# Second feed-forward output, parts 1 to 3: seven block products of 256 columns in place of plain 512-column products

## The chip, the cores and the metric

The kernel runs on one core of one Trainium2 chip. The metric is the device time of one execution in microseconds, as the median over runs of the same program. The engines are named as in the profile: PE (TensorE, with its weight loads as PEld), DVE (VectorE), ACT (ScalarE), POOL (GpSimd) and SP (SyncE, which here only issues DMAs).

## What is computed

The reference is one decoder block: a gated feed-forward, a token-mixing layer, a second gated feed-forward and a final norm, for 512 tokens of width 1024, in float32. What matters here is the second feed-forward:

```python
def swiglu(u, w_in, w_out):
    a, b = jnp.split(u @ w_in, 2, axis=-1)
    return (jax.nn.silu(a) * b) @ w_out

u = modulate(rmsnorm(h, g_norm_ffn2[l]), sh3, sc3)
h = h + 0.5 * gt3 * swiglu(u, w_ffn2_in[l], w_ffn2_out[l])
return rmsnorm(h, g_final)
```

The hidden width is 2816, that is 22 tiles of 128 rows; the output is 8 tiles of 128 rows; everything is held transposed, with the 512 tokens as columns.

## The kernel before

**Three matmuls for one.** A float32 product is made of three: each operand is split into a high part, rounded to the matmul's float32 form, and the low remainder. A product is high times high, high times low and low times high (`mm3`, L372 to L377, and L767 to L769 in `product`). The split of a weight chunk of 128 x 1024 is one ACT copy (L331, `whi`) and one DVE subtraction (L343, `wlo`) into a ring that has room for seven chunks. `look(n)` splits chunks up to n ahead of the one that PE takes next, `take` gives PE the next one.

**Block products.** The input half of the feed-forward (`u @ w_in`) runs from tile 4 on as `duo`, which makes two hidden tiles. It views weights, input and output as 2 x 2 blocks (512 rows each of the input, `a` and `b` of the output, 256 tokens each) and makes the product with seven block products in place of eight, by the Strassen-Winograd scheme: PE sums the seven in three PSUM banks A, B and C, ACT copies intermediate sums out (L774), and DVE adds them up (L807, L831). One block product is 24 matmuls of 256 columns and takes one weight chunk. Of the seven chunks of a set four are loaded; two more are sums that DVE makes (L268), and two are made by an adding DMA from POOL (L276), all ordered in `plan` by `blocks`. The sums of the input `u` are made once, as tiles `S`.

**Hidden tiles and parts.** After `duo` come `mult` (silu(a) times b, L793), `high` (ACT, L774, into `HI`) and `low` (DVE, L800, into `HK`). The 22 hidden tiles go into the output product in five parts, `PARTS = ((0, 4), (4, 8), (8, 12), (12, 16), (16, 22))`. The output product of a part is written in `ffn` (L907 to L931): per part 8 output tiles, 4 hidden tiles each, 3 matmuls of 512 columns for each pair, four weight chunks, and for each output tile one DVE operation that multiplies by the gate and adds into `H` (L923). One pair of hidden tiles more than the part needs is made ahead of parts 1 to 3 (`pairs_before`).

**What sets the order.** Each engine's order is written out by hand: `look`, `product`, `step` and the copies follow each other in the program, and `later(n, f)` puts a piece of work behind the n-th block product from now. All weight DMAs are issued from SP in the order of `plan`, as buffers come free. When a block product follows plain 512-column matmuls, `settle` (L381) puts one matmul of 240 columns ahead of it. Eight PSUM banks are there; six are in rotation through `nb()`.

Of the kernel before, what the change touches and what calls it, by code (L numbers as in the profile page):

```python
# [8 lines left out]
F32 = mybir.dt.float32  # L9
# [5 lines left out]
P = 128  # L15
T = 512
# [43 lines left out]
            for i, c in ((0, c0), (0, c1), (1, c1), (1, c0))]  # L60


def lay_ffn(w_in, w_out, first, plain):
# [13 lines left out]
    for k0, k1 in PARTS:  # L77
        for m in range(KT):
            outs.append(_fmajor(w_out[k0 * P:k1 * P], np.arange(m * P, (m + 1) * P)))
    n = KT * (len(PARTS) - 1)  # L80
    return ins, [np.concatenate(outs[i:i + 2], axis=1) for i in range(0, n, 2)] + outs[n:]

# [64 lines left out]
class Kernel:  # L147
# [6 lines left out]
    def plan(self):  # L154
        (i1, o1), mix, (i2, o2) = chunk_widths()
        self.chunks = []
        for name, ws in (("wf1i", i1), ("wf1o", o1), ("wmix", mix), ("wf2i", i2), ("wf2o", o2)):
            off, rec = 0, []
            for w in ws:
                rec.append((name, off, w))  # L160
                off += P * w
            self.chunks.append(rec)
        f1i, f1o, mx, f2i, f2o = self.chunks


        self.loads, self.order, self.last = [], [], {}
        self.shifted, self.adds = set(), {}

        def plain(recs):
            for r in recs:  # L170
                n = len(self.loads)
                self.loads.append(r)
                self.last[n] = len(self.order)
                self.order.append((r[2], n, ("raw", n), None))

        def blocks(recs, plus=False):
            n = len(self.loads)
            i = len(self.order)
            self.shifted.update(range(len(self.order), len(self.order) + 7))
            self.loads.extend(recs)  # L180
            r11, r12, r22, r21 = (("raw", n + i) for i in range(4))
            x0, x1 = ("x", 0), ("x", 1)
            add = OP.add if plus else OP.subtract
            x2 = x1 if plus else x0
            if plus:
                self.adds[i + 2], self.adds[i + 3] = (r12, r22, True), (x1, r21, False)
            for need, src, make in ((0, r11, None), (1, x0, (x0, r12, r11, add)), (2, x1, (x1, r22, x0, add)), (3, r21, None),
                                    (3, r12, (r12, r22, r12, not plus and add)), (3, r22, None),
                                    (3, x2, (x2, r21, x1, not plus and add))):
# [387 lines left out]
    def out_end(self, ms, ksrc, gate):  # L577
# [2 lines left out]
        v, g = nc.vector, nc.gpsimd  # L580
        tiles = {}
        A, Bh = slice(0, HT), slice(HT, T)
        rA, rB = self.B[6], self.B[7]
        self.held = self.pos

        def scaled(m, hs):
# [95 lines left out]

    def ffn_post(self, j, s, pb):
        nc = self.nc
        h = self.fw.tile([P, T], F32, name=("hf", "u3")[j % 2])
        nc.vector.tensor_tensor(h, s, pb, op=OP.mult)
        hh, hl = self.HH[j % NH], self.HL[j % NH]
        nc.scalar.activation(hh, h, AF.Copy)  # L690
        nc.vector.tensor_tensor(hl, h, hh, op=OP.subtract)

    def ffn_silu(self, j, pa):
        s = self.fw.tile([P, T], F32, name=("sl", "u2")[j % 2])
        self.nc.scalar.activation(s, pa, AF.Silu)
        return s

# [73 lines left out]
    def duo(self, n, j, first, last, extra):  # L771
# [13 lines left out]
        s = self.fw.tile([P, 2 * T], F32, name="sl")  # L785
        c = self.fw.tile([P, 2 * T], F32, name="hf")
        u2, u3, p5 = (self.fw.tile([P, T], F32, name=x) for x in ("u2", "u3", "p5"))
# [10 lines left out]
        def low():  # L798
            x = slice(j % NH * T, (j % NH + 2) * T)
            v.tensor_tensor(self.HLall[:, x], c, self.HHall[:, x], op=OP.subtract)  # L800
# [31 lines left out]
        if last:  # L832
            mult()
            high()
            low()
        else:
            self.later(1, mult)
            self.later(2, high)
            self.later(2, low)

    def ffn2(self):
        self.put, self.now = [], 0
        bk = [self.nb() for _ in range(4)]
        self.head(2, bk, AF.Silu)

# [15 lines left out]
        self.ready = True  # L861
        self.free += self.rawx[1:]

    def open_ffn(self):
# [4 lines left out]
        self.HH, self.HL = ([x[:, i * T:(i + 1) * T] for i in range(NH)] for x in (self.HHall, self.HLall))  # L869
        self.Xall = xp.tile([P, 4 * D], F32, name="X")  # L870
        a11, a21, a12, a22 = (self.Xall[:, i * D:(i + 1) * D] for i in range(4))
        self.U4, self.X, self.rawx = ((a11, a12), (a21, a22)), [a11, a21], [a12, a22]
# [11 lines left out]
    def ffn(self, n, j, last=None):  # L884
# [9 lines left out]

        for part, (k0, k1) in enumerate(PARTS):
            tail = part + 1 == len(PARTS)
            extra = 1
            while j < pairs_before(n, part):
                if j < PLAIN[n]:
                    self.ffn_pair(j, beside)  # L900
# [4 lines left out]
                    j += 2  # L905
            if n == 0:
                last = self.beside_out(part) or last  # L907
            nk = k1 - k0
            hk = [(self.HH[k % NH], self.HL[k % NH]) for k in range(k0, k1)]
            if not tail:  # L910
# [674 lines left out]
    def build(self):  # L1585
# [23 lines left out]
        self.cond = tl("cond", D)  # L1609
# [3 lines left out]
        self.cs = tl("cs", 2 * T)  # L1613
        self.cos, self.sin = self.cs[:, :T], self.cs[:, T:]
        tl("pad", 32)
        self.tr, self.pi = tl("tr", 5 * P), tl("pi", P, I32)
        self.B = [psum.tile([P, T], F32, name=f"bank{i}") for i in range(8)]
        self.banks, self.bi = self.B[:6], 0
        self.adat = {}
# [11 lines left out]
            self.ffn(0, FIRST)  # L1631
            self.sums.close()
        self.mix()
        with self.open_ffn() as self.f2:
            self.sums, self.retired = self.open_sums(), []
            self.ffn2()

# [140 lines left out]
def lay_inputs(x, c, positions, w_ada, b_ada, g_norm_ffn1, w_ffn1_in, w_ffn1_out, g_norm_mix, w_in, w_pool,  # L1778
# [4 lines left out]
    f1i, f1o = lay_ffn(A(w_ffn1_in)[0], A(w_ffn1_out)[0], FIRST, PLAIN[0])  # L1783
    f2i, f2o = lay_ffn(A(w_ffn2_in)[0], A(w_ffn2_out)[0], 0, PLAIN[2])
    wp = np.zeros((P, 2 * P), np.float32)
    for g in range(4):
        r = 64 * (g % 2)
# [30 lines left out]
```

## Time and profile before

| what | value |
|---|---|
| median of 3 runs | 992.41 us (991.48 to 993.05) |
| the profiled execution | 992.0 us |
| its span in the profile | 990.2 us |
| around the span | 1.8 us |
| granted PE clock, mean | 0.999 |
| matmuls in the built program | 6500, of which 14 are `settle` |

The profile of this page is of one execution. Busy times count matmuls that overlap each other once; the duration given for a matmul includes its passage through the pipeline, so the pace of a stream of matmuls is read from their starts. For PE, DVE and ACT a "start" of the next row may lie ahead of the end of the row before, too: instructions of one engine overlap a little.

### The profile page before, as it was taken

The numbers are of one execution on the slowest core, as the hardware profiler recorded it, in microseconds if no ns is written. First come the engines' busy times: TensorE is split into PE (matmuls) and PEld (weight loads), VectorE is DVE, ScalarE is ACT, GpSimd is POOL, SyncE is SP. The second block draws the span as 40 slices with busy tenths as digits, with TensorE's granted clock in tenths as the row PEclk, the third lists the DMA queues.
The fourth block names the chain that finished last, engine by engine and source line by source line (L and its number), as shares of the span: only waits on it lengthen the run. The fifth ranks groups of instructions, "written<-read, shape, count | busy, mean of one in ns | idle before, by whom it ended". The sixth has DMA issues, their size and how long they took to land.

```text
span 990.2 us, 16423 instructions
## 1 busy us (share of the span) xinstructions
PE 979.9 (99%) x6688; PEld 892.8 (90%) x6688; DVE 764.6 (77%) x1072; ACT 474.6 (48%) x712; POOL 45.5 (5%) x49
## 2 busy tenths in 40 slices
PE   8999999999999999999999999999999999999997
PEld 7888998989999899888879998998899898998997
DVE  7989979889797677888879877768676667566653
ACT  5453553525445553446545552455355254352553
POOL 0000000000000000006200000000010000000002
PEclk9999999999999999999999999999999999999999
DMA  9856445465563416654243326513576365563512
GB/s 345 277 184 241 150 149 178 163 192 160 186 205 105 141 57 194 229 184 161 68 122 111 107 81 212 175 44 106 145 194 174 88 175 140 128 184 80 152 34 86
DMA packets 47470, 151.19 MB, mean 153 GB/s; under 512 B 6561, under 2 KB 9377, under 8 KB 47394
## 3 DMA queue, kind: packets, MB, share of 16 engines
q1 hardware_dynamic: 44224, 140.18, 43.4%
q0 software_dynamic: 2592, 9.44, 5.5%
q8 instruction: 52, 0.85, 0.4%
q10 hardware_dynamic: 578, 0.53, 0.2%
q14 instruction: 24, 0.20, 0.1%
HBM read 135.29 MB, written 2.24 MB: 139 GB/s over the span
## 4 chain that ended last, share of the span: by engine, by line
PE 94%; DVE 2%; DMA 1%; SPq 1%; issue 1%; ACT 0%; POOL 0%; POOLq 0%; DVEq 0%; ACTq 0%
PE bank L375 15%; PE bank L376 15%; PE bank L377 15%; PE bank L769 13%; PE bank L768 13%; PE bank L767 13%; PE bank L1744 1%; PE bank L1748 1%; PE bank L1746 1%; SPq L1076 1%; PE bank L1420 1%; PE bank L1122 1%; PE bank L1173 1%; DMA H<-xT 1%; PE bank L1421 1%
## 5 line engine op out<-in xcount | busy, mean ns | idle before, releaser
L343 DVE TENSOR_TENSOR wlo<-raw,whi 128x1024 fp32r<-128x1024 f32 (+4 forms) x162 | 170.6, 1065 | 60.0 <-ACT whi L331 59.8
L767 PE MATMUL bank<-UH,whi 128*128 128x256 f32 x640 | 176.7, 276 | 0.0
L768 PE MATMUL bank<-UL,whi 128*128 128x256 f32 x640 | 176.7, 276 | 0.0
L769 PE MATMUL bank<-UH,wlo 128*128 128x256 f32 x640 | 176.7, 276 | 0.0
L331 ACT ACTIVATE whi<-raw 128x1024 fp32r<-128x1024 f32 (+4 forms) x162 | 146.2, 921 | 39.6 <-DVE raw L268 33.0
L375 PE MATMUL bank<-HI,whi 128*128 128x512 f32 (+1 forms) x406 | 146.2, 360 | 0.0
L376 PE MATMUL bank<-HK,whi 128*128 128x512 f32 (+1 forms) x406 | 145.9, 359 | 0.0
L377 PE MATMUL bank<-HI,wlo 128*128 128x512 f32 (+1 forms) x406 | 145.8, 359 | 0.0
L343 DVE TENSOR_TENSOR wlo<-X,whi 128x1024 fp32r<-128x1024 f32 (+3 forms) x104 | 111.9, 1083 | 39.6 <-ACT whi L331 39.4
L767 PEld LDWEIGHTS bank<-UH,whi 128*128 128x128 f32 x640 | 120.1, 188 | 0.4
L768 PEld LDWEIGHTS bank<-UL,whi 128*128 128x128 f32 x640 | 120.2, 188 | 0.0
L769 PEld LDWEIGHTS bank<-UH,wlo 128*128 128x128 f32 x640 | 120.1, 188 | 0.0
L767 PE MATMUL bank<-SH,whi 128*128 128x256 f32 x408 | 112.6, 276 | 0.0
L768 PE MATMUL bank<-SL,whi 128*128 128x256 f32 x408 | 112.6, 276 | 0.0
L769 PE MATMUL bank<-SH,wlo 128*128 128x256 f32 x408 | 112.6, 276 | 0.0
L331 ACT ACTIVATE whi<-X 128x1024 fp32r<-128x1024 f32 (+3 forms) x104 | 95.7, 943 | 24.9 <-DVE X L268 23.9
L375 PE MATMUL bank<-UH,whi 128*128 128x512 f32 (+1 forms) x304 | 105.6, 348 | 0.0
L376 PE MATMUL bank<-UL,whi 128*128 128x512 f32 (+1 forms) x304 | 104.2, 343 | 0.1
L377 PE MATMUL bank<-UH,wlo 128*128 128x512 f32 (+1 forms) x304 | 104.0, 342 | 0.0
L377 PEld LDWEIGHTS bank<-HI,wlo 128*128 128x128 f32 x406 | 76.2, 188 | 11.6
L375 PEld LDWEIGHTS bank<-HI,whi 128*128 128x128 f32 x406 | 76.2, 188 | 11.5
L376 PEld LDWEIGHTS bank<-HK,whi 128*128 128x128 f32 x406 | 76.3, 188 | 11.3
(350 smaller groups left out, 1831.0 us busy)
## 6 DMA issues: line engine op xcount, KB each, us to landing
raw<-wmix SPq DMA_DIRECT2D x44, 512.0 KB, 3.8
raw<-wf1i SPq DMA_DIRECT2D x31, 512.0 KB, 4.6
raw<-wf2i SPq DMA_DIRECT2D x30, 512.0 KB, 4.0
ada<-wada SPq DMA_DIRECT2D x23, 512.0 KB, 5.5
AR<-wada SPq DMA_DIRECT2D x19, 512.0 KB, 4.4
X<-wf2i SPq DMA_DIRECT2D x14, 512.0 KB, 4.1
cs<-wada SPq DMA_DIRECT2D x12, 512.0 KB, 3.7
X<-wf1i SPq DMA_DIRECT2D x12, 512.0 KB, 4.4
```

Source lines behind the costliest of these rows:

```text
L331: self.nc.scalar.activation(self.hi[:, y], r[:, x], AF.Copy)
L343: self.nc.vector.tensor_tensor(self.lo[:, y], r[:, x], self.hi[:, y], op=OP.subtract)
L375: M(ps, hi, uh, start=start, stop=False)
L376: M(ps, hi, ul, start=False, stop=False)
L377: M(ps, lo, uh, start=False, stop=stop)
L767: M(o, hi, uh, start=start and p == 0 and k == 0, stop=False, skip_group_check=True)
L768: M(o, hi, ul, start=False, stop=False, skip_group_check=True)
L769: M(o, lo, uh, start=False, stop=k == 3, skip_group_check=True)
L1076: nc.sync.dma_start(w[32 * o:32 * o + 32], t[32 * i:32 * i + 32])
L1122: nc.tensor.matmul(S[:, o], q[:, toks], k[:, ks], start=True, stop=True, skip_group_check=True)
L1173: self.nc.tensor.matmul(self.bO[64 * h:64 * h + 64, P * hp:P * hp + P], x, pt[:, (2 * h + j) * P:(2 * h + j + 1) * P], start=j == first, s ...
L1420: M(b, uh, hi, start=k == 0, stop=False)
```

## The change

Parts 1, 2 and 3 of the second feed-forward's output product are written with seven block products as well (`out_blocks`): a part's weights are seen as 2 x 2 blocks of 256 rows by 512 columns, the hidden tiles as blocks of 256 rows by 256 tokens. Each of the seven products is 24 matmuls of 256 columns (4 output tiles, 2 hidden tiles, 3 matmuls). All eight PSUM banks take part: A, B, C and a fourth pair U, two banks each. The block sums of the hidden tiles are made behind each `duo` of tiles 4 to 15 (`block_hidden`): four DVE operations of 256 columns, and one more high and low split of 768 columns into two new tiles `GI` and `GK`. The output of a part is taken up by ACT copies to banks and to a tile `ev`, four DVE additions, and twelve DVE operations into `H`. Parts 0 and 4 stay, and so does the first feed-forward.

The loads are the same in number and size; the weights are laid out in other blocks (`_out_blocks`), and the chunks of the three parts go through `blocks` in `plan`, with two DVE sums and two adding DMAs for each part. `settle` goes where a `duo` now follows block products (3 of 14). In the built program 288 matmuls of 512 columns are replaced by 504 of 256 columns (6713 in all). The tiles `sl`, `hf`, `u2`, `u3` and `p5` become slices of two tiles `wide` and `ev`. Four tiles that are used only up to the mixing layer (`cond`, `cs`, `tr`, `pi`) get a pool of their own that is closed before the second feed-forward. The negative gate for the lower half of the output is made by one DVE operation of 128 x 4 at the start of `ffn2`.

```diff
+BLOCK_PARTS = {0: (), 2: (1, 2, 3)}
...
-                plain(outs[part * KT // 2:(part + 1) * KT // 2] if part + 1 < len(PARTS) else outs[-KT:])
+                if part in BLOCK_PARTS[n]:
+                    blocks(outs[part * KT // 2:(part + 1) * KT // 2], True)
+                else:
+                    plain(outs[part * KT // 2:(part + 1) * KT // 2] if part + 1 < len(PARTS) else outs[-KT:])
...
+        part = next(i for i, (k0, k1) in enumerate(PARTS) if k0 <= j < k1)
+        then = self.block_hidden(j) if part in BLOCK_PARTS[n] else None
+        ends = [pairs_before(n, i) for i in BLOCK_PARTS[n]]
...
+        elif then:
+            for f in (mult, *then[:4]):
+                self.later(1, f)
+            for f in then[4:6]:
+                self.later(2, f)
+            for f in then[6:]:
+                self.later(4 if j + 2 in ends else 3, f)
...
+    def block_hidden(self, j):
...
+        return [sub(8, 4, 5), sub(3, 7, 5), minus(2, 3, 4), minus(5, 6, 2),
+                high(self.HHall[:, two], at(5, 4)), low(self.HLall[:, two], at(5, 4), self.HHall[:, two]),
+                high(self.G[0][:, one], at(2, 3)), low(self.G[1][:, one], at(2, 3), self.G[0][:, one])]
+
+    def out_blocks(self, k0):
...
+        A, B, C, U = x[:2], [x[2], spare[0]], [x[5], x[3]], [spare[1], x[4]]
+        self.banks, self.bi = C + B + A, 0
...
+        def gated(m, h, x):
+            y = self.H[m] if h is None else self.H[m][:, h * HT:(h + 1) * HT]
+            v.scalar_tensor_tensor(y, x, (gate if m < 4 else self.minus)[:, m % 4 if m > 3 else m:m % 4 + 1], y,
+                                   op0=OP.mult, op1=OP.add)
+
+        def lower(banks, h):
+            return lambda: [gated(m, h, banks[m // 2][:, m % 2 * HT:(m % 2 + 1) * HT]) for m in range(4)]
+
+        def sums(h, banks):
+            for i in range(2):
+                y = ev[:, 2 * i:2 * i + 2, h, :]
+                v.tensor_tensor(y, y, r(banks[i]), op=OP.add)
+
+        for i, (banks, u, start) in enumerate(((A, 6, True), (B, 5, True), (A, 4, False), (C, 1, False), (A, 3, False),
+                                               (B, 0, False), (A, 2, False))):
+            self.look(4)
+            w, uk = self.take(), blk(u)
+            for m in range(4):
+                o = banks[m // 2][:, m % 2 * HT:(m % 2 + 1) * HT]
+                for k in range(2):
+                    (hi, lo), (uh, ul) = w[2 * m + k], uk[k]
+                    M(o, hi, uh, start=start and m % 2 == 0 and k == 0, stop=False, skip_group_check=True)
+                    M(o, hi, ul, start=False, stop=False, skip_group_check=True)
+                    M(o, lo, uh, start=False, stop=k == 1, skip_group_check=True)
+            self.step()
+            for y in range(2):
+                if i == 0:
+                    copy(C[y], A[y])
+                elif i == 1:
+                    copy(ev[:, 2 * y:2 * y + 2, 1, :], r(B[y]))
+                elif i == 2:
+                    copy(ev[:, 2 * y:2 * y + 2, 0, :], r(A[y]))
+                elif i == 4:
+                    copy(U[y], A[y])
+            if i == 4:
+                lower(C, 0)()
+            elif i == 5:
+                sums(1, U)
+            elif i == 6:
+                sums(0, B)
+                for m in range(4):
+                    gated(4 + m, None, self.ev[:, m * T:(m + 1) * T])
+                self.later(1, lower(A, 1))
...
+        self.minus = self.mod[:, 0:4]
+        self.nc.vector.tensor_scalar(self.minus, self.mod[:, 68:72], -1.0, None, op0=OP.mult)
...
-            extra = 1
+            extra = 0 if part and part - 1 in BLOCK_PARTS[n] else 1
...
+            if part in BLOCK_PARTS[n]:
+                self.out_blocks(k0)
+                continue
```

More of the change, by code (lines that the diff above doesn't have):

```diff
@@ L60, in _blocks, with _out_blocks, lay_ffn @@
             for i, c in ((0, c0), (0, c1), (1, c1), (1, c0))]
-def lay_ffn(w_in, w_out, first, plain):
+def _out_blocks(w, k0):
+    rows = ((k0, k0 + 2), (k0 + 1, k0 + 3))
+    return [np.concatenate([w[k * P:(k + 1) * P, (4 * j + m) * P:(4 * j + m + 1) * P] for m in range(4) for k in rows[i]],
+                           axis=1) for i, j in ((0, 0), (0, 1), (1, 1), (1, 0))]
+def lay_ffn(w_in, w_out, first, plain, block_parts):
     ins, outs = [], []
@@ L76, in lay_ffn @@
         ins.extend(_blocks(w_in, 0, DFF, j))
[L77 to L81, printed above, removed]
+    for part, (k0, k1) in enumerate(PARTS):
+        if part in block_parts:
+            outs.extend(_out_blocks(w_out, k0))
+            continue
+        tiles = [_fmajor(w_out[k0 * P:k1 * P], np.arange(m * P, (m + 1) * P)) for m in range(KT)]
+        if part + 1 < len(PARTS):
+            tiles = [np.concatenate(tiles[i:i + 2], axis=1) for i in range(0, KT, 2)]
+        outs.extend(tiles)
+    return ins, outs
 POOLED = np.concatenate([np.arange(64) + 64 * g for g in (0, 2, 1, 3)])
@@ L582, in out_end @@
         A, Bh = slice(0, HT), slice(HT, T)
-        rA, rB = self.B[6], self.B[7]
+        rA, rB = (b for b in self.B if not any(b is x for x in self.banks))
         self.held = self.pos
@@ L681, in head, with work @@
         self.held = None
+    def work(self, name, w):
+        return self.wk[name][:, :w] if self.wk else self.fw.tile([P, w], F32, name=name)
     def ffn_post(self, j, s, pb):
         nc = self.nc
-        h = self.fw.tile([P, T], F32, name=("hf", "u3")[j % 2])
+        h = self.work(("hf", "u3")[j % 2], T)
         nc.vector.tensor_tensor(h, s, pb, op=OP.mult)
@@ L693, in ffn_silu @@
     def ffn_silu(self, j, pa):
-        s = self.fw.tile([P, T], F32, name=("sl", "u2")[j % 2])
+        s = self.work(("sl", "u2")[j % 2], T)
         self.nc.scalar.activation(s, pa, AF.Silu)
@@ L784, in duo @@
         A, B, C = self.nb(), self.nb(), self.nb()
-        s = self.fw.tile([P, 2 * T], F32, name="sl")
-        c = self.fw.tile([P, 2 * T], F32, name="hf")
-        u2, u3, p5 = (self.fw.tile([P, T], F32, name=x) for x in ("u2", "u3", "p5"))
+        s, c = self.work("sl", 2 * T), self.work("hf", 2 * T)
+        u2, u3, p5 = (self.work(x, T) for x in ("u2", "u3", "p5"))
         q = lambda x: x.rearrange("p (j h t) -> p j h t", j=2, h=2)
@@ new lines, in out_blocks, with blk @@
+    def out_blocks(self, k0):
+        nc, v, M = self.nc, self.nc.vector, self.nc.tensor.matmul
+        gate = self.mod[:, 64:72]
+        copy = lambda o, x: nc.scalar.activation(o, x, AF.Copy)
+        r = lambda x: x.rearrange("p (m t) -> p m t", m=2)
+        x = self.banks[self.bi % 6:] + self.banks[:self.bi % 6]
+        spare = [b for b in self.B if not any(b is y for y in x)]
+        A, B, C, U = x[:2], [x[2], spare[0]], [x[5], x[3]], [spare[1], x[4]]
+        self.banks, self.bi = C + B + A, 0
+        ev = self.ev.rearrange("p (m h t) -> p m h t", m=4, h=2)
+        def blk(i):
+            res = []
+            for j in (k0, k0 + 2):
+                if i < 4:
+                    y = slice((j % NH * 2 + i) * HT, (j % NH * 2 + i + 1) * HT)
+                    res.append((self.HHall[:, y], self.HLall[:, y]))
+                else:
+                    y = slice((j // 2 % 2 * 3 + i - 4) * HT, (j // 2 % 2 * 3 + i - 3) * HT)
+                    res.append((self.G[0][:, y], self.G[1][:, y]))
+            return res
+        def gated(m, h, x):
[38 more added lines that the diff above has]
+                self.later(1, lower(A, 1))
@@ L862, in more, with open_ffn @@
         self.free += self.rawx[1:]
-    def open_ffn(self):
+    def open_ffn(self, last=False):
         st = ExitStack()
```

30 lines of the change are left out of this document (24 added, 6 removed).

## The prediction

> **What bounds the kernel now.** I read the page first: the busy shares, then the chain that ended last.
>
> ```profile
> PE 979.9 (99%) x6688; PEld 892.8 (90%) x6688; DVE 764.6 (77%) x1072; ACT 474.6 (48%) x712; POOL 45.5 (5%) x49
> ...
> PE 94%; DVE 2%; DMA 1%; SPq 1%; issue 1%; ACT 0%; POOL 0%; POOLq 0%; DVEq 0%; ACTq 0%
> ```
>
> PE is 94% of the chain. A busy PE can still be a slow one, so the next question is whether it waits in the stage that is changed. The list of waits for the stretch 640 to 990 us has two lines for PE matmuls, and the larger is this one:
>
> ```profile
> PE bank L473 <- DVE r L468: 0.4, 1, 0.4
> ```
>
> That is the norm ahead of the stage, not the stage. So between 690 and 975 us PE runs from one matmul into the next, and the stage lasts as long as its matmuls. Their pace is in the PE timeline, in the starts (first column) of the first matmuls of each stretch:
>
> ```profile
> 709.41 0.28 PE L767 MATMUL bank<-UH,whi 128*128 128x256 f32 x1
> ...
> 766.54 0.40 PE L375 MATMUL bank<-HI,whi 128*128 128x512 f32 x1
> ...
> 788.43 0.28 PE L767 MATMUL bank<-UH,whi 128*128 128x256 f32 x1
> ...
> 826.53 0.40 PE L375 MATMUL bank<-HI,whi 128*128 128x512 f32 x1
> ...
> 848.42 0.28 PE L767 MATMUL bank<-UH,whi 128*128 128x256 f32 x1
> ...
> 886.51 0.40 PE L375 MATMUL bank<-HI,whi 128*128 128x512 f32 x1
> ...
> 908.41 0.28 PE L767 MATMUL bank<-UH,whi 128*128 128x256 f32 x1
> ```
>
> From 709.41 to 766.54 lie three sets of seven block products: 57.13 / 21 = 2.720 us for a product of 24 matmuls, 113.3 ns for a matmul of 256 columns. The output parts 1, 2 and 3 of 96 matmuls of 512 columns, each with the `settle` behind it, take 21.89, 21.89 and 21.90 us; 96 matmuls alone are about 21.76, so 226.7 ns each. A matmul of half the columns takes exactly half the time: nothing is paid per matmul, and the weight load of each is hidden at both sizes.
>
> **The change part by part.**
>
> *PE.* Each of the three parts has 7 products of 2.720 us = 19.04 us in place of 21.89 us, with the `settle` gone. That is 2.85 us a part, 8.55 us in all, if PE gets what it needs in time. The moving operand is now `HI`, `HK`, `GI` and `GK` at 256 columns; `HI` and `HK` are used at 256 columns already in the last part, with the same duration as `UH` (0.28 us, as in the starts above), in the rows by form from 946 us on:
>
> ```profile
> L376 PE MATMUL bank<-HK,whi 128*128 128x256 f32 x48 | 13.3, 277 | 0.0
> ```
>
> The Trainium skill, "TensorE: Matmul & The Clock Gate", section "Back-to-back issue gap", has a warm gap of N/2.4 + 2.5 ns, a fixed cost for each matmul. By it the 216 extra matmuls cost 0.5 us more than their columns, and the end would be 984.5 in place of 984.0. The starts above show none of it, and the sum stays with them.
>
> *DVE.* This is where the change puts work, so I add it up for one set of seven products, the time PE takes for it being 19.04 us. Rows by form, 709 to 946 us, with 768 and 256 columns as the nearest forms:
>
> ```profile
> L343 DVE TENSOR_TENSOR wlo<-X,whi 128x1024 fp32r<-128x1024 f32 x36 | 44.1, 1224 | 27.0 <-ACT whi L331 27.0
> L923 DVE SCALAR_TENSOR_TENSOR H<-bank,mod,H 128x512 f32<-128x512 f32 x25 | 18.5, 750 | 23.4 <-PE bank L377 23.4
> L268 DVE TENSOR_TENSOR X<-raw,X 128x1024 f32<-128x1024 f32 x8 | 9.8, 1219 | 0.0
> L800 DVE TENSOR_TENSOR HK<-hf,HI 128x1024 fp32r<-128x1024 f32 x8 | 9.7, 1218 | 0.2 <-ACT HI L774 0.2
> L831 DVE TENSOR_TENSOR hf<-u,bank 128x512 f32<-128x512 f32 x9 | 6.1, 680 | 0.0
> L343 DVE TENSOR_TENSOR wlo<-X,whi 128x768 fp32r<-128x768 f32 x2 | 1.9, 954 | 1.3 <-ACT whi L331 1.3
> ...
> L529 DVE SCALAR_TENSOR_TENSOR H<-bank,mod,H 128x256 f32<-128x256 f32 x10 | 4.8, 482 | 4.9 <-PE bank L377 4.9
> ```
>
> These durations overlap by some 0.09 us when instructions follow each other, as the starts show:
>
> ```profile
> 744.62 0.69 DVE L807 TENSOR_TENSOR hf<-u,p 128x512 f32<-128x512 f32 x1
> 745.23 1.22 DVE L343 TENSOR_TENSOR wlo<-X,whi 128x1024 fp32r<-128x1024 f32 x1
> 746.36 0.68 DVE L831 TENSOR_TENSOR hf<-u,bank 128x512 f32<-128x512 f32 x1
> ```
>
> So I count 1.13 us for 1024 columns, 0.87 for 768, 0.68 with the gate and 0.61 without for 512, 0.39 for 256. A `duo` today is 9 x 1.13 (seven splits, two sums) + 2 x 0.61 + 2 x 1.13 = 13.65 us; the window 709.0 to 766.5 below has 40.57 for three, 13.5 each. `block_hidden` adds 4 x 0.39 + 0.87 = 2.43, so 16.0 of 19.04 us. `out_blocks` is 9 x 1.13 + 8 x 0.39 + 4 x 0.61 + 4 x 0.68 = 18.45 of 19.04 us. It fits, with little to spare. That DVE may be this full is shown by the first feed-forward, in the second row:
>
> ```profile
> 709.00:766.50 57.50, 57.50 (x508) 57.42 (x507) 40.57 (x41) 32.28 (x43) 3.46 (x4) 1.00 0.63 172
> ...
> 95.00:120.00 25.00, 25.00 (x184) 23.52 (x183) 24.88 (x27) 12.99 (x17) 0.00 (x0) 1.00 0.45 141
> ```
>
> The columns are the stretch, its length, then busy us of PE, PEld, DVE, ACT and POOL, the granted clock, the DMA share and GB/s. DVE is busy for 24.88 of 25.00 us there, and PE never waits. Splits run four products (10.88 us) ahead of PE, and that is what takes such a stretch up.
>
> *ACT.* A part gets eight copies of 512 columns and three more weight copies, each `duo` a copy of 768. ACT was at 32.28 of 57.50 us; out of 19.04 us a part now has 7 x 1.05 + 8 x 0.60 + up to 1.9 for the last `duo`'s high parts = 14.1. The load is no matter; the order is. A copy of A behind product i must be done before product i + 2 writes A, and ACT works in order:
>
> ```profile
> 747.50 0.28 PE L767 MATMUL bank<-UH,whi 128*128 128x256 f32 x1
> ...
> 750.42 1.22 DVE L793 TENSOR_TENSOR hf<-sl,hf 128x1024 f32<-128x1024 f32 x1
> ...
> 751.87 1.05 ACT L774 ACTIVATE HI<-hf 128x1024 fp32r<-128x1024 f32 x1
> 753.20 0.60 ACT L774 ACTIVATE p<-bank 128x512 f32<-128x512 f32 x1 [0.28 <-PE bank L769]
> 753.69 1.06 ACT L331 ACTIVATE whi<-X 128x1024 fp32r<-128x1024 f32 x1
> 755.92 0.60 ACT L774 ACTIVATE u<-bank 128x512 f32<-128x512 f32 x1 [1.17 <-PE bank L769]
> ```
>
> The first row is the start of this `duo`. Its A copy (the last row) is done 9.0 us after that, and the fifth product, number 4, writes A at 4 x 2.72 = 10.88. With the change the `HI` copy waits for four more DVE operations, three of them each on the one before (0.39 + 3 x 0.48 = 1.8 us behind `mult`, the DVE row, which ends 4.1 us in). `HI` then runs from 6.0 to 7.0 us, the copies of B (two in a part, 0.50 from start to start as from 753.20 to 753.69) to 8.1, the weight copy to 9.0, the two copies of A to 10.1. PE needs A at 10.88: 0.8 us to spare in a part, 1.7 in a `duo`. By the same count the other bank hand-overs have more: `lower(C, 0)` ends some 17.2 us into the part and C is written at 19.04; `sums(0, B)` ends at 22.0 and the `duo`'s copy into that bank can start at 21.96, for a bank that PE writes at 27.2. So PE waits for none of them, and the 8.55 us stay; a miss costs what is missing, and its cover is gone when DVE or a weight copy is over 0.8 us late there.
>
> *POOL and DMA.* Three sets more need six more adding DMAs (24 for 18). Issue to landing, and the first, the last and two more of the 18 issues, those two for the set that starts at 747.50:
>
> ```profile
> raw<-raw POOLq DMA_DIRECT2D x3, 512.0 KB, 5.6
> ...
> 697.04 1.04 POOL L276 DMA_DIRECT2D raw<-raw  x1 [219.23 <-DMA raw<-wf2i]
> ...
> 738.46 0.86 POOL L276 DMA_DIRECT2D raw<-raw  x1 [11.56 <-DVE X L268]
> 745.07 0.86 POOL L276 DMA_DIRECT2D X<-X  x1 [5.74 <-DVE wlo L343]
> ...
> 925.43 0.86 POOL L276 DMA_DIRECT2D X<-raw  x1 [6.17 <-DVE wlo L343]
> ```
>
> The second has landed by 745.07 + 0.86 + 5.6 = 751.5, and ACT takes its chunk at 753.69: 2.2 us to spare today, about 4 with ACT later by 1.8. The loads on SP are the same in number, size and order; the DMA share of 0.63 in the row of 709 to 766 us is what three sets in a row cost, and no stretch asks for more. I cost this part at nothing.
>
> *Start of the stage.* The one DVE operation of 128 x 4 (L952 of the changed kernel) stands between the last addition of squares and the next norm step, which follow each other in the chain that ended last. Its nearest row is the 128 x 8 scaling of the same tile:
>
> ```profile
> 645.30 0.43 DVE AR L570
> 645.72 0.39 DVE ut L480
> ...
> L417 DVE TENSOR_SCALAR mod<-mod x2: 171/171/171, 88.9 to 623.9; 128x8 f32<-128x8 f32 x2
> ```
>
> At 0.17 us less the overlap it costs 0.1 us; the bounds are 0 and 0.17. The smaller pools and moved tiles have no instruction; I cost them at nothing, with no gain or loss beyond a wait at the first use of a moved tile, which comes 10 us after its last reader.
>
> *Sum.* -8.55 + 0.1 = -8.45 us. The profiled execution (992.0 us: span 990.2 and 1.8 around it) becomes 983.55, its span 981.75. The median shown, 992.41, is 0.4 us above that execution; I forecast the median: **984.0 us**.
>
> **The rivals.**
>
> *1. ACT's copies of A come late in the parts.* The margin of 0.8 us is an estimate out of ten terms, and two copies of 128 x 512 into halves of `ev` have no row of their own. If each of the three parts loses 1 to 1.5 us at product 4, it is 987 to 988.5. For it: DVE ahead of that point is the fullest place. Against it: the same chain in `duo` has 1.9 us to spare today.
>
> *2. The adding DMAs land late.* If a fuller DVE holds POOL up, the chunks made by POOL come late, ACT waits in order, and its copies with it. It takes 2.2 us to begin with; 1 us beyond that in each of three parts and six sets would be 9 us, and if two of three such misses reach PE it is 990. The POOL issues above take 0.86 us, but for the first with 1.04, whatever DVE does beside them. The Trainium skill, "SBUF — State Buffer", section "Who interferes with whom", says that a DVE instruction with two SBUF inputs contends with a GpSimd instruction that reads SBUF; the sums and low parts of `block_hidden` and the new splits have two. The even issue times speak against it here.
>
> *3. Slower: DVE stays bound to ACT's pace.* DVE was idle for 57.50 - 40.57 = 16.9 us in three sets, 5.6 each, mostly behind ACT's weight copies, which themselves stand behind copies that wait for PE. If that idle time does not shrink as work is added, a `duo` with `block_hidden` takes 16.0 + 5.6 = 21.6 us (2.6 over) and a part 24.1 (5.0 over): 6 x 2.6 + 3 x 5.0 = 30.6, less the lead of 10.9 = 19.7 us lost, 1003.7 us. It turns the gain into a loss when 4.4 of the 5.6 us stay (9 x 4.4 - 20.0 - 10.9 = 8.7). Without any overlap of DVE's instructions a part alone would be 9 x 1.22 + 8 x 0.48 + 4 x 0.68 + 4 x 0.75 = 20.5, also over 19.04, but the two sets between give that back. The stretch 95 to 120 us speaks against it: there the idle time went to 0.12 us.
>
> *4. The change does not do what it says.* The built program has 288 matmuls of 512 columns less, 504 of 256 columns more and 3 `settle` less, so the work is as counted. What could fail is the pace: with `G` and `HI` as moving operands 256 columns could take more than 113.3 ns. At 130 ns (504 x 16.7 ns = 8.4 us) the gain is gone, 992.4. The row of `HK` at 256 columns above speaks against it.
>
> **How the numbers follow.** Forecast 0.76 (983 to 985.5); rival 1 0.12 (985.5 to 989); rival 2 0.03 (about 990); rival 3 0.06 (from 994 up); rival 4 0.03 (about 992). The predicted time is the forecast's, 984.0. The range takes the forecast with the scatter of the runs shown (0.6 to 0.9 us either way) and rival 1: 982.8 to 988.5. About 0.2% (2 us) is what a measurement of this kernel tells from no change: faster is under 990.4, which holds for the forecast, rival 1 and part of rival 2: 0.89. Slower, over 994.4, is rival 3 and a share of 4: 0.07. Within: 0.04.
>
> **What would show it.** In the profile of the changed kernel the starts from the first product of a part to the first of the next `duo` should be 19.04 us apart; a gap inside, before the fifth product of a part, is rival 1, and the waits would name a bank of A against an ACT copy. DVE should be at about 16 us for a set with `block_hidden` and 18.4 for a part, with its idle time behind ACT's weight copies well under 5 us a set; if that stays, rival 3. POOL issues above 1 us, or ACT waiting for a DMA by POOL, would be rival 2. A spacing other than 113 ns inside a product would be rival 4. The forecast is wrong if PE waits for more than 2 us in all between 700 and 940 us.

## The result, and the profile after

The changed kernel takes **982.45 us** (median; 982.34 to 982.67), the kernel before in the same rounds 991.94 us (991.48 to 993.05): a ratio of 0.9909, 95% interval 0.9897 to 0.9921. The forecast was 984.0 with a range from 982.8, so the time lies 0.35 us below the range's lower end. The profiled executions have spans of 980.9 and 990.2 us, 9.3 apart.

First the page of the changed kernel, busy shares and chain by engine:

```profile
PE 971.9 (99%) x6901; PEld 895.7 (91%) x6901; DVE 802.7 (82%) x1144; ACT 500.0 (51%) x753; POOL 50.7 (5%) x55
...
PE 94%; DVE 2%; SPq 1%; issue 1%; ACT 1%; POOL 0%; DMA 0%; POOLq 0%; ACTq 0%; DVEq 0%
```

DVE has 38 us more work and PE 8 us less, and PE still makes up 94% of the chain. The waits of PE matmuls between 640 and 960 us are down to one line, and it lies in the norm ahead of the stage:

```profile
PE bank L488 <- DVE r L483: 0.5, 1, 0.5
```

The starts of the first matmuls of each stretch, from PE's timeline (start, duration, line):

```profile
708.74 0.28 PE L785 MATMUL bank<-UH,whi 128*128 128x256 f32 x1
...
765.87 0.28 PE L926 MATMUL bank<-GI,whi 128*128 128x256 f32 x1
...
784.91 0.28 PE L785 MATMUL bank<-UH,whi 128*128 128x256 f32 x1
...
822.99 0.28 PE L926 MATMUL bank<-GI,whi 128*128 128x256 f32 x1
...
842.03 0.28 PE L785 MATMUL bank<-UH,whi 128*128 128x256 f32 x1
...
880.11 0.28 PE L926 MATMUL bank<-GI,whi 128*128 128x256 f32 x1
...
899.15 0.28 PE L785 MATMUL bank<-UH,whi 128*128 128x256 f32 x1
...
937.23 0.40 PE L390 MATMUL bank<-HI,whi 128*128 128x512 f32 x1
```

Each block part takes 19.04 us (21.89 before), each pair of sets 38.08. From the first set to the last part it is 228.49 us; before, 709.41 to 946.50 is 237.09. So 8.60 of the 9.3 us are won here, against 8.55 in the sum. The load of the stage, as busy us of PE, PEld, DVE, ACT and POOL:

```profile
784.91:822.99 38.08, 38.08 (x338) 38.08 (x337) 35.09 (x43) 20.80 (x28) 4.01 (x5) 1.00 0.69 172
822.99:842.03 19.04, 19.04 (x170) 19.04 (x169) 16.47 (x22) 14.47 (x20) 1.19 (x2) 1.00 0.63 156
```

Two sets and a part together hold 51.56 us of DVE in 57.12 us. Summed by the prediction they were 2 x 16.0 + 18.45 = 50.5; some of a part's work falls into the set behind it (the last four operations into `H` among it), which is why the rows alone read 17.5 for a set and 16.5 for the part. DVE is idle for 5.56 us per three sets of products.

One thing is there that the stage did not have before: shortly before the end of the first part and of the second, ACT waits for a chunk that an adding DMA of POOL makes:

```profile
783.71 1.07 ACT L346 ACTIVATE whi<-raw 128x1024 fp32r<-128x1024 f32 x1 [1.29 <-DMA raw<-X]
...
840.80 1.06 ACT L346 ACTIVATE whi<-raw 128x1024 fp32r<-128x1024 f32 x1 [1.26 <-DMA raw<-raw]
```

The first of these DMAs was issued at 777.55. PE has no wait behind either.

The rest of the difference is small and lies in two places. PE's wait in the norm ahead of the stage is 0.46 us against 0.38 (the negated gate, +0.08). And 0.7 us arose before 17 us, where the first feed-forward begins:

```profile
15.63 1.65 PE L1867 MATMUL bank<-UH,whi 128*128 128x512 f32 x6 [0.48 <-ACT UH L507]
```

Before, that row starts at 16.36. Whether the moved tiles do this is the first thing the experiments ask.

### The profile page after: what moved, and what is told of

It is laid out like the page before. It is cut to its first block, busy times and chain, and to the rows that moved or that the text cites. A ratio compares the mean times of both kernels' runs of the same rounds, so it can differ in the third digit from the quotient of the medians.

```text
span 980.9 us, 16987 instructions
## 1 busy us (share of the span) xinstructions
PE 971.9 (99%) x6901; PEld 895.7 (91%) x6901; DVE 802.7 (82%) x1144; ACT 500.0 (51%) x753; POOL 50.7 (5%) x55
## 4 chain that ended last, share of the span: by engine, by line
PE 94%; DVE 2%; SPq 1%; issue 1%; ACT 1%; POOL 0%; DMA 0%; POOLq 0%; ACTq 0%; DVEq 0%
PE bank L390 13%; PE bank L787 13%; PE bank L785 13%; PE bank L786 13%; PE bank L391 13%; PE bank L392 13%; PE bank L928 2%; PE bank L926 2%; PE bank L927 2%; PE bank L1867 2%; PE bank L1871 1%; PE bank L1869 1%; SPq L1195 1%; PE bank L1539 1%; PE bank L1241 1%; PE bank L1292 1%
## 5 line engine op out<-in xcount | busy, mean ns | idle before, releaser
L358 DVE TENSOR_TENSOR wlo<-X,whi 128x1024 fp32r<-128x1024 f32 (+3 forms) x119 | 122.9, 1048 | 21.9 <-ACT whi L346 21.7
L346 ACT ACTIVATE whi<-X 128x1024 fp32r<-128x1024 f32 (+3 forms) x119 | 106.0, 915 | 25.1 <-DVE X L283 24.5
L390 PE MATMUL bank<-HI,whi 128*128 128x512 f32 (+1 forms) x310 | 108.9, 351 | 0.0
L391 PE MATMUL bank<-HK,whi 128*128 128x512 f32 (+1 forms) x310 | 108.5, 350 | 0.0
L392 PE MATMUL bank<-HI,wlo 128*128 128x512 f32 (+1 forms) x310 | 108.4, 350 | 0.0
L785 PEld LDWEIGHTS bank<-SH,whi 128*128 128x128 f32 x408 | 76.6, 188 | 0.0
L786 PEld LDWEIGHTS bank<-SL,whi 128*128 128x128 f32 x408 | 76.6, 188 | 0.0
L787 PEld LDWEIGHTS bank<-SH,wlo 128*128 128x128 f32 x408 | 76.6, 188 | 0.0
```

Source lines behind the costliest of these rows:

```text
L346: self.nc.scalar.activation(self.hi[:, y], r[:, x], AF.Copy)
L358: self.nc.vector.tensor_tensor(self.lo[:, y], r[:, x], self.hi[:, y], op=OP.subtract)
L390: M(ps, hi, uh, start=start, stop=False)
L391: M(ps, hi, ul, start=False, stop=False)
L392: M(ps, lo, uh, start=False, stop=stop)
L785: M(o, hi, uh, start=start and p == 0 and k == 0, stop=False, skip_group_check=True)
```

## The experiments

All gaps and distances below are read from PE's timeline of the run's profile, as above; medians are of the run's rounds.

**The start-up: the kernel before again, and the pool alone.** The first is the kernel before, unedited; the second has

```
-        self.cond = tl("cond", D)
+        self.cond = el("cond", D)      # el: the pool "early"; cs, tr, pi likewise
...
         self.mix()
+        early.close()
```

> The kernel before, unchanged, as a second sample. Between the two profiles at hand 0.75 us of the difference arose before 16 us, where the first feed-forward's first matmul started at 16.36 us (before) and 15.63 us (after). Theory (scatter of when the first loads land): this run's start lies anywhere between 15.6 and 16.4 us, and its times between 991.4 and 993.1 us. Rival (the new place of the moved tiles starts the program earlier): the start is 16.3 to 16.4 us again, in every run of this kernel.

> The kernel before with one edit of the change alone: the four one-phase tiles (cond, cs, tr, pi) in an own pool that is closed after the middle stage. No instruction differs. Theory: within 0.3 us of the kernel before over the rounds, the first feed-forward's start anywhere between 15.6 and 16.4 us. Rival: 0.6 to 0.8 us faster (991.2), with the start at 15.6 us.

Measured: 991.43 us (990.82 to 991.96) and 991.35 us (990.94 to 991.75); before, in the same rounds, 991.50 us over 29 runs (ratios 0.9997, interval 0.9988 to 1.0006, and 0.9998, 0.9989 to 1.0006). The first feed-forward starts at 15.44 us in the first, in the second at:

```profile
15.76 1.43 PE L1748 MATMUL bank<-UH,whi 128*128 128x512 f32 x5 [0.48 <-ACT UH L492]
```

The unedited kernel moved its own start from 16.36 to 15.44 us, a little below the 15.6 expected. Over all fourteen profiles of this study the start lies between 15.04 and 16.36 us, with and without the pool. It is scatter: the moved tiles cost and win nothing that can be seen, and 0.7 us of the distance of the two profiles does not belong to the change.

**One part alone.**

```
-BLOCK_PARTS = {0: (), 2: (1, 2, 3)}
+BLOCK_PARTS = {0: (), 2: (2,)}
```

> The changed kernel with only part 2 as block products; parts 1 and 3 plain, with their sums not formed. Theory (each part gives 2.85 us by itself, PE never waits): 21.89 to 19.04 us in part 2, nothing elsewhere but the 0.1 us of the sign operation ahead of the stage: 2.75 us faster than before by the matmuls, 989.2 with the start as in the kernel before, 988.4 with the earlier start. Rival (part of the gain is given by the three parts together, through the lead of the splits): other than 2.7 to 2.9 us between the first product of part 2 and that of the next set.

Measured: 988.80 us against 991.50, ratio 0.9973 (0.9961 to 0.9984), 2.7 us. Part 2 runs from 826.06 to 845.10, 19.04 us; parts 1 and 3 stay at 21.89, and PE has no gap. The parts add up; none lives off another.

**The sums alone.** `block_hidden` in every set, plain output parts; the output of these parts is another one, the amounts of work are as said.

```
-            if part in BLOCK_PARTS[n]:
+            if part in ():
                 self.out_blocks(k0)
```

> The cost of the sums alone: every set of parts 1 to 3 forms the sums of block_hidden (four more operations of 256 columns, one low part of 768, one high part of 768), but the parts multiply plainly, as in the kernel before. HI and HK hold other combinations of the hidden blocks there, so the output of these parts is another one; amounts of work are as said. Theory (sums lie beside PE): no PE wait in the stage, the time of the kernel before plus 0.1 us for the sign operation, 992.0 to 992.2. Rival (DVE is bound to ACT's pace and each added microsecond on DVE shows): 6 sets times 2.4 us less the lead of up to 10.9 us, so 995 to 1006 us.

Measured: 991.27 us against 991.50, ratio 0.9998 (0.9989 to 1.0007). DVE in a pair of sets, then in the part behind it:

```profile
788.25:826.34 38.09, 38.09 (x338) 38.09 (x337) 28.09 (x32) 20.66 (x28) 1.73 (x2) 1.00 0.58 160
826.34:848.13 21.79, 21.79 (x99) 18.03 (x97) 15.66 (x20) 7.35 (x9) 1.74 (x2) 1.00 0.45 108
```

Before, the same stretches (788.43 to 826.53 and on to 848.32) have 24.83 and 14.14 us of DVE. That is 4.8 us more for two sets (the sum had 2 x 2.43 = 4.9), and none of it reaches PE: first set to last part is 237.10 us, before 237.09. The first half of rival 3 falls here.

**How full may DVE be?** Every seventh split, then three of seven, done twice in parts 1 to 3:

```
             self.nc.vector.tensor_tensor(self.lo[:, y], r[:, x], self.hi[:, y], op=OP.subtract)
+        if <every 7th | 3 of 7>:
+            for y, x in parts:
+                self.nc.vector.tensor_tensor(self.lo[:, y], r[:, x], self.hi[:, y], op=OP.subtract)
```

> The changed kernel with every seventh weight split on DVE done twice from part 1 to part 3 (the same result again, output unchanged): about 9 operations of 1.13 us more, 3.4 us for each three sets of 57.1 us, in which DVE is idle 5.6 us. Theory (DVE takes up its idle time, PE is the only bound): no PE wait, 982.4. Rival (what idle time DVE has left behind ACT stays as work is added): 3.4 us for each of three parts less a lead of 3 to 9 us, so +1 to +7 us.

> The same with three of seven splits done twice: 10.2 us more for each three sets, 4.6 us more than DVE's idle time. Theory (DVE becomes the bound once its idle time is full): 3 times 4.6 = 13.9 us less the lead of 3 to 9 us, +5 to +11 us, 987 to 993, with DVE near 100% in parts 1 to 3. Rival (idle time stays): +21 to +28 us. If neither, under +3 us, DVE was not the next bound.

Measured: 982.76 us (982.37 to 983.73) and 999.27 us (998.45 to 1000.04). The same stretch of the first and of the second:

```profile
823.00:880.00 57.00, 57.00 (x505) 57.00 (x504) 54.92 (x67) 35.26 (x48) 5.21 (x6) 1.00 0.64 166
```

```profile
823.00:880.00 57.00, 54.26 (x465) 53.47 (x464) 55.90 (x67) 30.82 (x42) 5.18 (x6) 1.00 0.58 141
```

With DVE at 54.92 of 57.00 us PE waits for nothing and the stage takes 228.49 us to the hundredth. DVE's idle time does shrink as work is added: rival 3 is refuted. With three of seven DVE is at 98%, and PE waits:

```profile
PE bank L792 <- ACT ev L799: 4.1, 4, 1.7
PE bank L792 <- ACT bank L799: 2.3, 2, 1.2
PE bank L792 <- DVE H L914: 2.1, 2, 1.1
PE bank L933 <- ACT ev L892: 1.1, 2, 0.9
```

These are all of PE's waits in the stage, and none is for a split: 7.5 of the 9.6 us are for banks that ACT copies, 2.1 for banks that DVE reads. ACT in its turn waits mostly for DVE there, 54 us in its three longest rows (750 to 950 us). So late bank hand-overs, rival 1's mechanism, come first when DVE overflows; but only 1.1 us of them lie in the parts (L933), where rival 1 placed them, and 8.5 in the sets (L792). The cost is 16.8 us over the changed kernel, above the 5 to 11 expected; the stage from first set to last part takes 244.65 us, 16.2 more. By the starts, the eleven gaps of PE sum to 11.5 us of these; the first matmul behind each is 0.22 us ahead of the next in place of 0.11, which is 1.2 us more. (If the overflow was the 13.9 us forecast, the lead absorbed about 1 us, not 3 to 9.) The other 3.5 us come from something not expected at all, to which the next runs lead.

**The margin of the copies of A.** One, two and three operations of 1024 columns ahead of the sums of the last set before a part (the run with two was made when the other two were known):

```
+            more = [lambda: v.tensor_tensor(s, c, c, op=OP.add)] * 3 if j + 2 in ends else []
-            for f in (mult, *then[:4]):
+            for f in (mult, *more, *then[:4]):
```

> The changed kernel with one DVE operation of 1024 columns more (s <- c + c, overwritten later, so the output is the same) ahead of the sums of the last set before each of the three parts. It makes the HI copy on ACT 1.13 to 1.22 us later, and with it, in order, the copies of A that product 4 of the part waits for. The changed kernel's profile has these copies done 1.04 us before that product. Theory (the margin is real and about 1 us): a PE gap of 0.1 to 0.2 us ahead of product 4 of each part, +0.3 to +0.6 us in all, 982.8 to 983.0. Rival (ACT has other slack, or PE's bound is elsewhere): no gap, 982.4.

> The changed kernel with two DVE operations of 1024 columns more ahead of the sums in the last set before a part (s <- c + c, output unchanged). One such operation gave no gap, three gave a gap of 2.17 us at the first and 1.75 at the second part, and none at the third, whose last set forms no sums and so is not delayed. Theory (what counts is the copy of A's first bank, 1.5 us ahead of product 4 in the changed kernel, since product 4 writes the second bank 1.36 us later): gaps of 0.7 to 0.9 us at two parts, 1.6 us in all, up to 2 us more each if PE's clock drops or its pace goes to 117.8 ns behind the gap: 984 to 988. Rival (the margin is the 1.04 us to the end of both copies): 1.2 to 1.4 us each, and one late operation should have shown a gap.

> The same with three such operations, 3.4 to 3.7 us. Theory: a gap of 2.35 to 2.6 us ahead of product 4 of each of the three parts, +7.0 to +7.9 us, 989.5 to 990.4; the waits name a bank of A behind an ACT copy. Rival (slack elsewhere): under +3 us.

First ACT in the first block part of the changed kernel, which starts at 765.87, and then, from PE's timeline, the start of its product 4:

```profile
771.76 1.06 ACT L875 ACTIVATE HI<-wide 128x1024 fp32r<-128x1024 f32 x1 [1.36 <-DVE wide L874]
772.73 1.06 ACT L885 ACTIVATE ev<-bank 128x512 f32<-128x512 f32 x2
773.68 1.06 ACT L346 ACTIVATE whi<-X 128x1024 fp32r<-128x1024 f32 x1
774.63 1.08 ACT L885 ACTIVATE ev<-bank 128x512 f32<-128x512 f32 x2
```

```profile
776.75 0.28 PE L926 MATMUL bank<-HI,whi 128*128 128x256 f32 x1
```

`HI` runs from 5.9 to 7.0 us into the part, the copies of B to 7.9, the weight copy to 8.9, the two of A to 9.84: each within 0.3 us of the count (7.0, 8.1, 9.0, 10.1). But the row of A holds two copies (x2). Product 4 writes the first bank at 10.88 and the second only half a product, 1.36 us, later. The first copy ends some 0.5 us earlier, near 9.36, so the margin is about 1.52 us and not the 0.8 of the prediction.

Measured: 983.12 us, 986.03 us and 991.65 us (989.08 to 994.75). By the starts of the copies of A, counted from the start of the part, they are 1.13, 2.39 and 3.65 us late. With one late operation there is no gap, as a margin of 1.52 us has it; the expectation of 0.1 to 0.2 us was from the end of both copies, and wrong. The stage takes 228.49 us in that run as well (709.08 to 937.57), so the 0.67 us of its median over the changed kernel do not come from the stage. The first gap with two and with three:

```profile
777.10 0.39 PE L927 MATMUL bank<-HI,whi 128*128 128x256 f32 x1 [0.76 <-ACT ev L886]
```

```profile
779.92 0.39 PE L927 MATMUL bank<-HI,whi 128*128 128x256 f32 x1 [2.01 <-ACT ev L886]
```

From the last matmul of product 3 the gaps are 0.93 and 2.17 us, against 2.39 - 1.52 = 0.87 and 3.65 - 1.52 = 2.13. Two of the three parts show gaps; the third has none, since the set before it belongs to the last part and forms no sums, which the expectation of the first of these runs had missed.

The gaps do not explain the times. In the third run they are 3.9 us; the stage is longer by 7.92 (709.74 to 946.15, 236.41). Besides the slow first matmul, two other things stand behind a gap:

```profile
780.48:783.90 3.42, 3.42 (x18) 3.42 (x17) 3.42 (x5) 2.99 (x4) 0.87 (x1) 0.50 0.46 162
...
780.00:784.00 4.00, 4.00 (x21) 4.00 (x22) 4.00 (x5) 3.47 (x5) 0.87 (x1) 0.57 0.56 187
784.00:790.04 6.04, 6.04 (x53) 6.04 (x52) 6.04 (x11) 3.65 (x5) 0.81 (x1) 1.00 0.69 158
790.04:829.62 39.58, 39.58 (x339) 39.58 (x338) 34.69 (x42) 20.67 (x28) 3.51 (x5) 1.00 0.65 167
```

Behind the 2.17 us the granted clock (third column from the end) is 0.50 for 3.42 us, which costs about 1.7 us. No other gap in these runs, up to 1.9 us, did that. The Trainium skill, "TensorE: Matmul & The Clock Gate", section "What's actually happening", lets an idle window of about 3.4 us, free-running, halve the clock; the half clock agrees with it, but here a gap of 2.17 us was enough.

Then, at a granted clock of 1.00, two sets take 39.58 us in place of 38.08. All their matmuls are slower, by mean duration in the groups by form of this stretch and of the changed kernel:

```profile
L785 PE MATMUL bank<-SH,whi 128*128 128x256 f32 x48 | 13.5, 281 | 0.0
```

```profile
L785 PE MATMUL bank<-SH,whi 128*128 128x256 f32 x48 | 13.2, 276 | 0.0
```

39.58 / 336 = 117.8 ns from start to start in place of 113.3, 4% more, with no gap between. It lasts until the next gap, at 840.80, behind which it is 113.3 again. In the run with two late operations the pace is slow from its first gap to its second, 502 matmuls or about 2.3 us. In the run with three of seven splits the pace changes for good at three of the eleven gaps (slow behind 819.36 and 883.07, fast behind 841.14), and at the others it is fast again within a few matmuls. PE has **two paces** for matmuls of 256 columns. That gave the sharper question: what does `settle` do?

**`settle` left out before, and kept after.**

```
-            extra = 1                                   # before.py
+            extra = 0 if n == 2 and part > 1 else 1
...
-            extra = 0 if part and part - 1 in BLOCK_PARTS[n] else 1     # changed kernel
+            extra = 1
```

> The kernel before without the short matmul (settle, 240 columns) behind output parts 1 to 3: a part of the change done alone. In two experiments a gap of PE was followed by a stretch in which every matmul of 256 columns took 117.8 ns in place of 113.3, until another gap. Theory (settle is only a matmul of 0.11 us, as the prediction counted it): -0.3 us, sets of products 19.04 us each as before, 991.2. Rival (it keeps PE in its faster pace where widths change): the sets behind the parts at 117.8 ns, 19.8 us each, +1.5 us for each of three stretches of two sets, so up to +4.5 us, 996.

> The changed kernel with settle kept behind the three block parts. Theory (0.11 us each and nothing else): +0.3 us, 982.8, all products at 113.3 ns. Rival (between matmuls of one width it shifts PE out of its faster pace): sets behind the parts at 117.8 ns, up to +4.5 us, 987.

Measured: 995.75 us against 991.62, ratio 1.0043 (1.0031 to 1.0056), so 4.1 us slower with a matmul less in three places; and 986.66 us (986.43 to 988.08), 4.2 us above the changed kernel, for three matmuls of 0.11 us. Both rivals hold. By the profiles, from first set to last part it is 241.22 us in the first run (before 237.09) and 232.58 in the second (changed 228.49), so both differences arise in the stage. The first sets behind a plain part without `settle`, and the next part:

```profile
788.41 0.28 PE L767 MATMUL bank<-UH,whi 128*128 128x256 f32 x1
...
827.99 0.40 PE L375 MATMUL bank<-HI,whi 128*128 128x512 f32 x1
...
849.77 0.28 PE L767 MATMUL bank<-UH,whi 128*128 128x256 f32 x1
```

39.58 us for two sets (three times), 21.78 for the plain part: in these three places 256 columns straight behind 512 start in the slow pace; 512 columns showed one pace only. With `settle` behind the block parts:

```profile
784.58 0.27 PE L396 MATMUL bank<-UH,whi 128*128 128x240 f32 x1
784.69 0.28 PE L785 MATMUL bank<-UH,whi 128*128 128x256 f32 x1
...
824.26 0.28 PE L926 MATMUL bank<-GI,whi 128*128 128x256 f32 x1
...
844.05 0.28 PE L396 MATMUL bank<-UH,whi 128*128 128x240 f32 x1
844.16 0.28 PE L785 MATMUL bank<-UH,whi 128*128 128x256 f32 x1
...
882.26 0.28 PE L926 MATMUL bank<-GI,whi 128*128 128x256 f32 x1
...
901.30 0.27 PE L396 MATMUL bank<-UH,whi 128*128 128x240 f32 x1
901.42 0.28 PE L785 MATMUL bank<-UH,whi 128*128 128x256 f32 x1
...
940.99 0.40 PE L390 MATMUL bank<-HI,whi 128*128 128x512 f32 x1
```

The first `settle` puts PE into the slow pace (39.57 us to 824.26, and 19.79 for the part behind), the second back into the fast one (38.10), the third into the slow one again (39.57). The short matmul is a switch: in these places it mends the pace where widths change, and where they do not it changes the pace each time.

**The negated gate elsewhere.** The 128 x 4 operation moved behind the first plain matmuls of the stage.

```
-        self.nc.vector.tensor_scalar(self.minus, self.mod[:, 68:72], -1.0, None, op0=OP.mult)
...
     def more(self):
+        self.nc.vector.tensor_scalar(self.minus, self.mod[:, 68:72], -1.0, None, op0=OP.mult)
```

> The changed kernel with the one operation that negates the gate (128 x 4) moved from the start of the second feed-forward to behind its first plain matmuls, where PE does not wait for DVE. Theory (it stands on the chain of the norm at the start): -0.08 us, 982.4, PE's wait in that norm back from 0.46 to 0.38 us. Rival (it costs nothing where it stands): 0.46 us again. Over the rounds this is at the edge of what can be told; the wait in the profile decides.

Measured: 982.40 us (981.83 to 984.35), the changed kernel's time as far as can be told. PE's wait in the norm:

```profile
649.24 0.71 PE L488 MATMUL bank<-cst,r 128*128 128x128 f32 x4 [0.38 <-DVE r L483]
```

0.38 us, as before the change: the operation costs 0.08 us where it stands. The profiled execution is the one of 984.35 us. It shows where such a single longer run comes from: its first two sets of the first feed-forward, which no edit touches, run from 102.62 to 142.13 us, 39.51 in place of 38.09, in the slow pace from the third product on (108.1 us), 1.4 of the 1.95 us by which it exceeds the median. The profiles of the runs with one late operation and of `settle` left out have such a stretch as well, some 143 matmuls from 361 us on, 0.55 us, and no edit touches them. What changed the pace there is not shown.

## Why the prediction came out as it did, point by point

- **PE is the bound, and a product keeps 2.720 us.** Right. Three parts of 19.04 us; 8.60 us between the same marks, forecast 8.55; one part alone gave its share. That 256 columns take exactly half the time of 512 holds in the fast pace alone, and the rows before showed no other in this stage.
- **`settle` gone.** The number was right, the step was not understood. It was counted as three matmuls of 0.11 us. Leaving it out of the kernel before costs 4.1 us, keeping it in the changed one 4.2. That the parts now have 256 columns like the sets is what makes it superfluous, and leaving it out was a condition for the 8.55 us, not a term of 0.3 in them. Rival 4 named a pace above 113 ns as a danger, but looked for it in new operands and not in the change of widths.
- **DVE fits.** Right: 51.56 us of 57.12, the sum 50.5. Rival 3 is refuted by the sums alone (no cost) and by DVE at 96% without a wait of PE. It does turn slower once DVE overflows, by PE waiting for banks, mostly those that ACT copies.
- **The order of ACT has room.** Right in each term to 0.3 us; the margin itself was undersized, 1.52 us in place of 0.8, because product 4 needs only the first bank of A at its start. The runs with two and three late operations gave the gaps of 0.93 and 2.17 us that this margin leaves. Rival 1's mechanism exists and its price was too low: a miss costs the gap, 0.11 us at the first matmul behind it, in two of four cases about 2.2 us by the pace until the next gap, and in one of them 1.7 us by the clock.
- **Adding DMAs cost nothing.** The price was right, the reason was not. PE has no wait in the stage with 24 of them, and POOL's issues took 0.85 to 0.89 us but for the first. But the room of 2 to 4 us was counted for one chunk only: two others came late, and ACT waited 1.29 and 1.26 us for them, the sign that the prediction gave for rival 2. The DMA share rose to 0.69, above the 0.63 that it took for the most. What such waits would cost with less room ahead of PE was not tried.
- **The negated gate 0.1 us, the moved tiles nothing.** Right: 0.08 us, by the wait and by moving it; the pool alone 0.9998.
- **The level.** The move was forecast as -8.45 and is -8.52 by the trace's own marks (-8.60 + 0.08). The medians moved by 9.49 us, and the forecast's 1.55 us too much come from elsewhere: the three runs of before on which it stands had a median of 992.41, while later ones had 991.50 (29 runs), 991.58 and 991.62. That is 0.8 to 0.9 us. The last 0.6 us or so is not settled: it is within the start-up's scatter of 1.3 us over the profiles and that of the pace ahead of the stage (0.55 us in two profiles), and the kernel before told from itself by rounds leaves 0.9988 to 1.0006.

## What to carry to other kernels

Where PE is the bound, count its starts before and after: a product's pace, its number, and whether anything stands in the gap between; the rest is whether DVE and ACT stay ahead, which is a matter of order and not of load until DVE is almost full. A margin is counted to the first bank that is needed, not to the last. And a tiny matmul that looks like waste, or a gap of half a microsecond, can decide the pace of the hundreds of matmuls behind it: compare the mean duration of one form in two stretches before calling an instruction free.

## What the runs showed of the hardware that was not expected

- Matmuls of 256 columns with a weight load each run at 113.3 or at 117.8 ns from start to start (276 or 281 ns in the groups), both at a granted clock of 1.00. A pace can hold for tens of microseconds. A change from 512 to 256 columns led into the slow one in three places of three; a matmul of 240 columns between stretches of 256 switched in three of three, and of the 15 gaps of PE the three in the slow pace led back to the fast one, while of the twelve in the fast one four led to the slow one (0.93 to 2.17 us) and eight did not (0.22 to 1.32 us). 512 columns showed 226.7 ns only. What in PE holds this state is not shown.
- The Trainium skill, "TensorE: Matmul & The Clock Gate", section "Back-to-back issue gap", gives for a matmul by itself, at full clock, a gap from one to the next of N/2.4 + 2.5 ns. By that figure 256 columns would take an estimated 109.2 ns. No stretch of 256 columns here showed that, and one formula can't give two paces; the measured ones decide.
- The first matmul behind each of the 15 gaps of 0.2 to 2.2 us was 0.22 to 0.23 us ahead of the next in place of 0.11.
- One gap of 2.17 us was followed by 3.42 us at a granted clock of 0.50; fourteen gaps of 0.2 to 1.9 us were not.
